# Expert weights in rows of 8192 bytes, a ring of 12 places, and the next gather ahead of the down projection

## Chip, cores and metric

The kernel runs on one core of one Trainium2 chip. The metric is the device time of one execution in microseconds (us).

## The reference

One decoder layer on 256 tokens of 2048 features, all in float32. The part that the change touches is the channel half, a mixture of 32 experts in 4 groups: each token takes its best group and the two best experts in it.

```python
def hier_moe(h, w_grp, w_exp, w1, w3, w2):
    ht = h.reshape(-1, D)                                   # 256 x 2048
    pg = softmax(ht @ w_grp); g_sel = argmax(pg); p_g = max(pg)
    el_sel = logits (ht @ w_exp) of the 8 experts of g_sel
    top_p, top_i = lax.top_k(softmax(el_sel), 2)
    top_w = top_p / sum(top_p) * p_g                        # combine: 256 x 32, two entries a row
    for e in range(32):
        a = jax.nn.silu(ht @ w1[e]) * (ht @ w3[e])          # w1, w3: 2048 x 512
        y = y + combine[:, e:e + 1] * (a @ w2[e])           # w2: 512 x 2048
```

Ahead of it stand adaLN conditioning (`c` times a 2048 x 12288 matrix), an input projection, sparse attention beside a pooling branch, and an output projection. The three expert arrays are 384 MiB of the 554 MB that the core reads.

## The kernel before

Everything up to the router runs in stages: adaLN sums on VectorE, projections on TensorE, attention, pooling, the output projection with the router's logits built block by block (`route_block`, L530 to L566). Then L574 to L649 select experts and give each token a slot (at most 32 tokens, `CAP`, per expert) with each of its experts.

The experts run four at a time (`quad`, L663, eight calls at L801). One quad has these steps. **Gather**: VectorE builds a 0/1 matrix `gq` (L666 to L669); TensorE multiplies the tokens `x1c` with it (L676) into PSUM tiles of two banks (`banks`, tag `b2`, two of them); VectorE scales them into `xg` (L680). **Hidden**: for each block `kb` of 256 features and for `w1` and `w3`, two loads of 1 MiB bring 256 rows of two experts each (L694), and 8 float32 matmuls follow, four experts side by side in column groups of 32 (L699; the trace has two records for each matmul); the two results stand in the two one-bank PSUM tiles `mm`. **Turn**: SiLU, product, four transposes (L706 to L712). **Down** (`cols`): for 1024 output columns, over four blocks `f` of 128 hidden features, two loads of 1 MiB (two experts, 1024 columns each, L721) and 16 matmuls (L726). **Combine**: times the gate (L732), back to the tokens through `gwT` (L735, into `b2` tiles), added onto the residual `xs` (L737). The last quad takes its columns as 1024, 512, 256, 256 and stores each piece.

A load of weights needs a free place. `moe_w` (L655) hands places out: 13 of `FIRST_SLOTS` for the first 13 loads, then a ring of the 8 `MOE_SLOTS`. A place comes free when the last matmul that reads it is done. SyncE (SP) issues all weight loads in one fixed order and stands still at one whose place isn't free. The order on each engine is set when the kernel is built, by a list scheduler that may take a ready instruction ahead of one that waits; a tile's release follows all its readers.

In HBM an expert's `w1` row (512 floats) is 2048 bytes, and a partition takes two neighbouring rows (`r=2`), so a DMA row is 4096 bytes; of `w2` it is 1024 columns, also 4096 bytes. The order of features within `xg`, `x1c`, `wr`, `sc2T` and `sh2T` follows this `r`.

```python
    MOE_SLOTS = [(t, one) for t in ("Pq", "Pp", "H1")] + [("w", wp)] * 4 + [("H0", one)]
    FIRST_SLOTS = MOE_SLOTS + [("B8", one), ("acc", rot)] + [("f", fp)] * 3
```

Of the kernel before, what the change touches and what calls it, by code (L numbers as in the profile page):

```python
# [9 lines left out]
F32 = mybir.dt.float32  # L10
# [6 lines left out]
P = 128  # L17
# [17 lines left out]
CAP = 32  # L35
QE = 4
# [41 lines left out]
def layer_kernel(ctx: ExitStack, tc: tile.TileContext, x, c, w_ada, b_ada, norm1_g, w_in, q_norm_g,  # L78
# [20 lines left out]
    MOE_SLOTS = [(t, one) for t in ("Pq", "Pp", "H1")] + [("w", wp)] * 4 + [("H0", one)]  # L99
    FIRST_SLOTS = MOE_SLOTS + [("B8", one), ("acc", rot)] + [("f", fp)] * 3  # L100
# [97 lines left out]
    vb2 = one.tile([24, 256], F32, name="vb2")  # L198
    nc.sync.dma_start(vb2[0:8], norm2_g[0].rearrange("(k n) -> k n", n=256))
    nc.sync.dma_start(vb2[8:24], b_ada[3 * D:5 * D].rearrange("(k n) -> k n", n=256))  # L200
    pt = bank([P, 2, 24], "sm")
    for r in range(2):
        nc.tensor.transpose(pt[:, r], vb2.rearrange("k (q r) -> k r q", r=2)[:, r], ident[0:24, 0:24])
    v2T = one.tile([P, 24, 2], F32, name="v2T")
# [32 lines left out]
    def vec_end(acc, bias, gain, name):  # L237
        av = acc.rearrange("p (k q r) -> p k r q", q=P, r=2)
        pt = bank([P, KC], "fl")
        for k in range(KC):  # L240
            nc.tensor.matmul(pt[:, k:k + 1], lhsT=av[:, k // 2, k % 2], rhs=ones[:, 0:1], start=True, stop=True)  # L241
# [10 lines left out]
    def fill_steps():  # L252
        v2 = lambda j: v2T[:, 8 * j:8 * j + 8].rearrange("p k r -> p (k r)")
# [259 lines left out]
    wr = one.tile([P, 8, 2, 36], F32, name="wr")  # L513
    for r in range(2):
        nc.sync.dma_start(wr[:, :, r, 0:NE], w_exp.rearrange("(k p r) e -> p k r e", p=P, r=2)[:, :, r])
        nc.sync.dma_start(wr[:, :, r, NE:36], w_grp.rearrange("(k p r) e -> p k r e", p=P, r=2)[:, :, r])
# [11 lines left out]
    x1c = one.tile([P, NT, 8, 2, P], F32, tag="N", name="x1c")  # L528

    def route_block(n):  # L530
        if n == 3:
            while "sh2T" not in results:
                fill(1)
            sh2T = results["sh2T"]
            pb = bank([P, 36], "sm")
            for k in range(KC):
                nc.tensor.matmul(pb, lhsT=sh2T[:, k:k + 1].to_broadcast([P, P]), rhs=wr[:, k // 2, k % 2],
                                 start=(k == 0), stop=(k == KC - 1))
            nc.vector.tensor_copy(brt, pb)
        for i in range(NT):  # L540
            t = t2()
            nc.scalar.activation(t, xs[:, i, n * 512:(n + 1) * 512], AF.Square, accum_out=ss2[:, i, n:n + 1])
        xv = xs[:, :, n * 512:(n + 1) * 512].rearrange("p i (k q r) -> p i k r q", q=P, r=2)
        for i in range(NT):
            nc.scalar.copy(x1c[:, i, 2 * n:2 * n + 2], xv[:, i])
        pt = banks([P, 4, S])
        for u in range(4):
            for i in range(NT):
                nc.tensor.transpose(pt[:, u, i * P:(i + 1) * P], xv[:, i, u // 2, u % 2], ident)
        h = r4([P, 4, S])  # L550
        for u in range(4):
            k = n * 4 + u
            if u % 2:
                nc.vector.tensor_scalar(h[:, u], pt[:, u], sc2T[:, k:k + 1], None, op0=ALU.mult)
            else:
                nc.scalar.activation(h[:, u], pt[:, u], AF.Copy, scale=sc2T[:, k:k + 1])
        pl = bank([P, NT, 36], "sm")
        for i in range(NT):
            for u in range(4):
                k = n * 4 + u  # L560
                nc.tensor.matmul(pl[:, i], lhsT=h[:, u, i * P:(i + 1) * P], rhs=wr[:, k // 2, k % 2],  # L561
                                 start=(u == 0), stop=(u == 3))
# [100 lines left out]
    def quad(e0, last):  # L663
# [7 lines left out]
        for kq in range(2):  # L671
            px = banks([P, 8, QS])
            for u in range(8):
                k = kq * 8 + u
                for i in range(NT):
                    nc.tensor.matmul(px[:, u], lhsT=x1c[:, i, k // 2, k % 2],  # L676
                                     rhs=gq[:, i].rearrange("p e s -> p (e s)"), start=(i == 0), stop=(i == NT - 1))
# [8 lines left out]
        if e0 == 0:  # L686
            fill(100)
        hs = [bank([P, DE], "mm") for _ in range(2)]
        for kb in range(KC // 2):
            for wx, h in ((w1, hs[0]), (w3, hs[1])):  # L690
                ws = []
                for e in range(0, QE, 2):
                    w = moe_w([P, 2, 2, DE])
                    nc.sync.dma_start(w, wx[e0 + e:e0 + e + 2, kb * 256:(kb + 1) * 256, :].rearrange("e (p r) n -> p e r n", r=2))  # L694
                    ws += [w[:, 0], w[:, 1]]
                for r in range(2):
                    k = kb * 2 + r
# [14 lines left out]
        nc.vector.tensor_copy(aT, pa)  # L712

        def cols(c0, width):
# [14 lines left out]
            for n in range(0, width, 512):  # L729
                m = min(512, width)  # L730
                y = t2()
                nc.vector.tensor_mul(y[:, 0:m], py[:, n:n + m], gt2[:, c0 + n:c0 + n + m])  # L732
                pz = banks([P, NT, 512])
                for i in range(NT):
                    nc.tensor.matmul(pz[:, i, 0:m], lhsT=gwT[:, i], rhs=y[:, 0:m], start=True, stop=True)  # L735
                xv = xs[:, :, c0 + n:c0 + n + m]
                nc.vector.tensor_add(xv, xv, pz[:, :, 0:m])  # L737
                if last:
                    nc.scalar.dma_start(out[:, c0 + n:c0 + n + m].rearrange("(i p) n -> p i n", p=P), xv)

        cols(0, 1024)
        if last:
            cols(1024, 512)
            cols(1536, 256)
            cols(1792, 256)
        else:
            cols(1024, 1024)

# [1 line left out]
    def overflow():  # L750
        gt2 = results["gt2"]
        h2 = []
        for hf in range(2):
            h2T = slot([P, 8, S], FILL_SLOTS)
            x1n = wtile([P, NT, 8, P])
            for i in range(NT):
                nc.vector.tensor_scalar(x1n[:, i], x1c[:, i, hf * 4:hf * 4 + 4].rearrange("p k r q -> p (k r) q"), rs2[:, i:i + 1], None, op0=ALU.mult)
# [9 lines left out]
        with tc.For_i(0, NE, 1) as ev:  # L767
# [69 lines left out]
```

## Time and profile before

| | us |
|---|---|
| median of 3 runs | 1453.95 |
| lowest, highest | 1449.43, 1456.39 |
| span of the profiled execution | 1453.5 |
| TensorE busy in it | 1097.4 |
| VectorE busy in it | 476.8 |
| mean DMA rate over it | 383 GB/s |

The profile cuts the span into 40 slices of 36 us. Up to slice 12 TensorE and VectorE are busy; from slice 14 (about 500 us) on the experts run, and the DMA rate stands near 405 GB/s up to the last slices. The chain of work that ended last is for 57% of the span a load of expert weights.

### The profile page before, as it was taken

Reading aid. Unit: us, or ns where it says so; the run is one execution under the profiler, and the core shown is the slowest. Engines: PE = TensorE matmul, PEld = TensorE weight load, DVE = VectorE, ACT = ScalarE, POOL = GpSimd, SP = SyncE. Lnnn points to the kernel's source line nnn. Section 1 sums busy time; section 2 is a strip of 40 time slices with the busy share of each in tenths; the row PEclk is TensorE's granted clock in tenths of the full one; section 3 lists DMA queues with packets and bytes.
Section 4 is the critical chain, followed back from the end, with each engine's and each line's share of the span. In section 5 each row is a group of like instructions: output and inputs, shape, how many; then the busy total and the mean of one; then the engine's idle time right before and its main releaser. Section 6 shows DMA issues by size and latency. Waiting matters only on the chain.

```text
span 1453.5 us, 12826 instructions
## 1 busy us (share of the span) xinstructions
PE 1097.4 (75%) x5165; PEld 418.2 (29%) x5165; DVE 476.8 (33%) x815; ACT 99.7 (7%) x230; POOL 0.2 (0%) x4
## 2 busy tenths in 40 slices
PE   2999999999995867656867755675685677668655
PEld 1444444655564113111311311131131131113111
DVE  5876678996767003001201200210120021012002
ACT  3200002441220000000000000000000000000000
POOL 0000000000000000000000000000000000000000
PEclk9999999999976889999989999999999998899897
DMA  9999999999987999999999999999999999999997
GB/s 305 372 386 358 369 347 351 373 355 376 406 334 270 374 404 401 409 407 404 404 409 404 405 409 409 405 400 409 408 406 409 407 404 389 408 399 384 410 398 258
DMA packets 171968, 557.29 MB, mean 383 GB/s; under 512 B 15129, under 2 KB 29433, under 8 KB 163457
## 3 DMA queue, kind: packets, MB, share of 16 engines
q1 hardware_dynamic: 170544, 554.32, 98.5%
q10 hardware_dynamic: 1360, 2.10, 0.4%
q8 instruction: 43, 0.70, 0.2%
q14 instruction: 21, 0.16, 0.0%
HBM read 554.29 MB, written 2.10 MB: 383 GB/s over the span
## 4 chain that ended last, share of the span: by engine, by line
DMA 60%; PE 35%; DVE 4%; ACT 1%; issue 1%; SPq 0%; DVEq 0%
DMA w<-in_w_dram 57%; PE mm L395 11%; PE mm L503 8%; PE mm L699 6%; PE b L726 3%; DVE bacc L160 2%; DMA w<-in_w_ada_dram 1%; PE b L676 1%; DVE acc L160 1%; PE fl L233 1%; PE fl L232 1%; DMA w<-in_w_in_dram 1%; PE b L735 1%; PE fl L241 1%; PE sm L561 1%
## 5 line engine op out<-in xcount | busy, mean ns | idle before, releaser
L699 PE MATMUL mm<-w,xg 128*32 128x512 f32 x2048 | 364.2, 653 | 181.9 <-DMA w<-in_w_dram 181.9
L726 PE MATMUL b<-w,t 128*32 128x512 f32 (+1 forms) x1056 | 188.8, 642 | 98.6 <-DMA w<-in_w_dram 92.3
L395 PE MATMUL mm<-w,hT 128*128 128x512 f32 (+1 forms) x512 | 208.3, 563 | 3.2 <-ACT hT L386 1.7
L699 PEld LDWEIGHTS mm<-w,xg 128*32 128x32 f32 x2048 | 72.6, 113 | 467.1 <-DMA w<-in_w_dram 287.8
L707 DVE TENSOR_TENSOR t<-t,mm 128x512 f32<-128x512 f32 x8 | 5.5, 688 | 534.6 <-PE mm L699 470.1
L160 DVE SCALAR_TENSOR_TENSOR acc<-w,sT,acc 128x2048 f32<-128x2048 f32 x60 | 140.7, 2345 | 1.1 <-DMA w<-in_w_ada_dram 1.0
L395 PEld LDWEIGHTS mm<-w,hT 128*128 128x128 f32 x512 | 92.3, 193 | 106.4 <-issue 98.8
L732 DVE TENSOR_TENSOR t<-b,gt 128x512 f32<-128x512 f32 (+1 forms) x33 | 20.9, 671 | 269.7 <-PE b L726 269.7
L726 PEld LDWEIGHTS b<-w,t 128*32 128x32 f32 x1056 | 35.7, 113 | 242.4 <-DMA w<-in_w_dram 182.0
L160 DVE SCALAR_TENSOR_TENSOR bacc<-w,sT,bacc 128x512 f32<-128x512 f32 (+1 forms) x150 | 94.3, 643 | 10.8 <-DMA w<-in_w_ada_dram 8.0
L735 PE MATMUL b<-t,gwT 128*128 128x512 f32 (+1 forms) x132 | 62.5, 616 | 13.8 <-DVE t L732 13.8
L706 ACT ACTIVATE t<-mm 128x512 f32<-128x512 f32 x8 | 4.8, 597 | 865.5 <-PE mm L699 865.5
L676 PE MATMUL b<-gq,x1c 128*128 128x128 f32 x512 | 60.9, 282 | 1.7 <-DVE gq L669 1.7
L676 PEld LDWEIGHTS b<-gq,x1c 128*128 128x128 f32 x512 | 60.1, 198 | 2.1 <-DVE gq L669 2.1
L503 PE MATMUL mm<-w,mixA 128*128 128x512 f32 x128 | 59.3, 617 | 0.0
L503 PE MATMUL mm<-w,mixP 128*128 128x512 f32 x128 | 56.2, 592 | 0.0
L680 DVE TENSOR_SCALAR xg<-b,sc2T,sh2T 128x128 f32<-128x128 f32 x128 | 42.3, 404 | 24.2 <-PE b L676 24.2
L737 DVE TENSOR_TENSOR xs<-xs,b 128x1024 f32<-128x1024 f32 (+1 forms) x33 | 39.2, 1188 | 30.9 <-PE b L735 30.9
L735 PEld LDWEIGHTS b<-t,gwT 128*128 128x128 f32 x132 | 24.6, 197 | 55.7 <-DVE t L732 32.9
L503 PEld LDWEIGHTS mm<-w,mixA 128*128 128x128 f32 x128 | 24.6, 198 | 28.0 <-issue 28.0
L503 PEld LDWEIGHTS mm<-w,mixP 128*128 128x128 f32 x128 | 24.0, 190 | 27.4 <-issue 27.0
L401 DVE TENSOR_TENSOR pqkv<-pqkv,mm 128x512 f32<-128x512 f32 x24 | 16.5, 686 | 18.0 <-PE mm L395 17.9
(208 smaller groups left out, 459.1 us busy)
## 6 DMA issues: line engine op xcount, KB each, us to landing
w<-in_w_dram SPq DMA_DIRECT2D x380, 1024.0 KB, 16.7
w<-in_w_ada_dram SPq DMA_DIRECT2D x96, 1024.0 KB, 8.3
w<-in_w_in_dram SPq DMA_DIRECT2D x21, 1024.0 KB, 7.2
w<-in_w_out_dram SPq DMA_DIRECT2D x16, 1024.0 KB, 8.3
w<-in_w_in_dram SPq DMA_DIRECT2D x14, 512.0 KB, 8.7
w<-in_w_dram SPq DMA_DIRECT2D x8, 512.0 KB
xs<-in_x_dram SPq DMA_DIRECT2D x2, 1024.0 KB, 7.9
out_dram<-xs ACTq DMA_DIRECT2D x3, 512.0 KB, 8.4
```

The costliest lines, as they stand in the source:

```text
L160: nc.vector.scalar_tensor_tensor(acc, w[:, kk], sT[:, k:k + 1], acc, op0=ALU.mult, op1=ALU.add)
L232: nc.tensor.matmul(pt, lhsT=ones, rhs=acc[:, n * 512:(n + 1) * 512], start=True, stop=False)
L395: nc.tensor.matmul(po[:, :width], lhsT=hTs[k // 8][:, k % 8, i * P:(i + 1) * P], rhs=w[:, j], start=(j == 0), stop=(j == nk - 1))
L401: nc.vector.tensor_add(d, d, po[:, :width])
L503: nc.tensor.matmul(po, lhsT=mix[:, k, i * P:(i + 1) * P], rhs=ws[k // 4][:, k % 4], start=(k == 0), stop=(k == 7))
L676: nc.tensor.matmul(px[:, u], lhsT=x1c[:, i, k // 2, k % 2], rhs=gq[:, i].rearrange("p e s -> p (e s)"), start=(i == 0), stop=(i == NT - 1))
L680: nc.vector.tensor_scalar(xg[:, k], px[:, u], sc2T[:, k:k + 1], sh2T[:, k:k + 1], op0=ALU.mult, op1=ALU.add)
L699: nc.tensor.matmul(h[e * CAP:(e + 1) * CAP, :], lhsT=xg[:, k, e * CAP:(e + 1) * CAP], rhs=ws[e][:, r], start=(k == 0), stop=(k == KC - 1), ...
L726: nc.tensor.matmul(py[e * CAP:(e + 1) * CAP, nw], lhsT=aT[:, f, e * CAP:(e + 1) * CAP], rhs=ws[e][:, nw], start=(f == 0), stop=(f == 3), s ...
L732: nc.vector.tensor_mul(y[:, 0:m], py[:, n:n + m], gt2[:, c0 + n:c0 + n + m])
L735: nc.tensor.matmul(pz[:, i, 0:m], lhsT=gwT[:, i], rhs=y[:, 0:m], start=True, stop=True)
L737: nc.vector.tensor_add(xv, xv, pz[:, :, 0:m])
```

## The change

- `RB = 4`: a partition takes four neighbouring rows of `w1` and `w3`, so one load of 1 MiB is 512 rows of one expert, in DMA rows of 8192 bytes; a step of `hidden` is four loads and 16 matmuls, for twice as many features. All tensors in the order of features follow (`x1c`, `wr`, `v2T`, `vec_end`, `route_block`); the router's weights come in eight loads, not four.
- `down` loads whole rows of `w2` (2048 columns, 8192 bytes) of one expert, four loads a step, and keeps both `b2` tiles for the sums of all 2048 columns; `combine` then uses the `mm` banks for its products. The last quad (`down_last`) keeps its column pieces and their loads.
- The ring has 12 places: the 8, three places `f` and one `acc`.
- `gather` of the next quad stands between `hidden` and `down` of this one.

```diff
+RB = 4
-    MOE_SLOTS = [(t, one) for t in ("Pq", "Pp", "H1")] + [("w", wp)] * 4 + [("H0", one)]
-    FIRST_SLOTS = MOE_SLOTS + [("B8", one), ("acc", rot)] + [("f", fp)] * 3
+    MOE_SLOTS = [(t, one) for t in ("Pq", "Pp", "H1")] + [("w", wp)] * 4 + [("H0", one)] + [("f", fp)] * 3 + [("acc", rot)]
+    FIRST_SLOTS = MOE_SLOTS[:8] + [("B8", one), ("acc", rot)] + [("f", fp)] * 3
...
-        xv = xs[:, :, n * 512:(n + 1) * 512].rearrange("p i (k q r) -> p i k r q", q=P, r=2)
-        for i in range(NT):
-            nc.scalar.copy(x1c[:, i, 2 * n:2 * n + 2], xv[:, i])
+        xv = xs[:, :, n * 512:(n + 1) * 512].rearrange("p i (q r) -> p i r q", q=P, r=RB)
+        for i in range(NT):
+            nc.scalar.copy(x1c[:, i, n], xv[:, i])
...
-        for kb in range(KC // 2):
+    def hidden(e0, xg):
         hs = [bank([P, DE], "mm") for _ in range(2)]
+        for kb in range(KC // RB):
             for wx, h in ((w1, hs[0]), (w3, hs[1])):
                 ws = []
-                for e in range(0, QE, 2):
-                    w = moe_w([P, 2, 2, DE])
-                    nc.sync.dma_start(w, wx[e0 + e:e0 + e + 2, kb * 256:(kb + 1) * 256, :].rearrange("e (p r) n -> p e r n", r=2))
-                    ws += [w[:, 0], w[:, 1]]
-                for r in range(2):
-                    k = kb * 2 + r
+                for e in range(QE):
+                    w = moe_w([P, RB, DE])
+                    nc.sync.dma_start(w, wx[e0 + e, kb * RB * P:(kb + 1) * RB * P, :].rearrange("(p r) n -> p r n", r=RB))
+                    ws.append(w)
+                for r in range(RB):
+                    k = kb * RB + r
...
+    def combine(py, c0, m, gwT, store):
+        gt2 = results["gt2"]
+        y = t2()
+        nc.vector.tensor_mul(y[:, 0:m], py, gt2[:, c0:c0 + m])
+        for i in range(NT):
+            pz = bank([P, 512], "mm")
+            nc.tensor.matmul(pz[:, 0:m], lhsT=gwT[:, i], rhs=y[:, 0:m], start=True, stop=True)
+            xv = xs[:, i, c0:c0 + m]
+            nc.vector.tensor_add(xv, xv, pz[:, 0:m])
...
+    def down(e0, aT, gwT):
+        py = [banks([P, 1024]) for _ in range(2)]
+        for f in range(4):
+            ws = []
+            for e in range(QE):
+                w = moe_w([P, D])
+                nc.sync.dma_start(w, w2[e0 + e, f * P:(f + 1) * P, :])
+                ws.append(w)
+            for n in range(4):
+                for e in range(QE):
+                    nc.tensor.matmul(py[n // 2][e * CAP:(e + 1) * CAP, (n % 2) * 512:(n % 2 + 1) * 512],
...
+        for n in range(4):
+            combine(py[n // 2][:, (n % 2) * 512:(n % 2 + 1) * 512], n * 512, 512, gwT, False)
...
+    xg, gwT = gather(0)
+    fill(100)
     for q in range(NQ):
-        quad(q * QE, q == NQ - 1)
+        a = hidden(q * QE, xg)
+        if q == 0:
+            gate_end(5, results["gt2 sums"], "gt2")
+        held = gwT
+        if q + 1 < NQ:
+            xg, gwT = gather((q + 1) * QE)
+            down(q * QE, turned(a), held)
+        else:
+            down_last(q * QE, turned(a), held)
```

## Rows read from the trace of the kernel before

**Rows 1.** The page: busy time; granted clock, DMA share, DMA rate over 40 slices.

```profile
PE 1097.4 (75%) x5165; PEld 418.2 (29%) x5165; DVE 476.8 (33%) x815; ACT 99.7 (7%) x230; POOL 0.2 (0%) x4
...
PEclk9999999999976889999989999999999998899897
DMA  9999999999987999999999999999999999999997
GB/s 305 372 386 358 369 347 351 373 355 376 406 334 270 374 404 401 409 407 404 404 409 404 405 409 409 405 400 409 408 406 409 407 404 389 408 399 384 410 398 258
```

**Rows 2.** The chain that ended last: start us, us, what.

```profile
606.03 1.94 PE mm L699 x12
...
626.51 1.94 PE mm L699 x12
...
689.06 1.94 PE b L726 x12
...
1312.19 3.60 PE b L726 x12
```

**Rows 3.** The page: DMA issues of expert weights, count, KB each, us to landing.

```profile
w<-in_w_dram SPq DMA_DIRECT2D x380, 1024.0 KB, 16.7
...
w<-in_w_dram SPq DMA_DIRECT2D x8, 512.0 KB
```

**Rows 4.** DMA packets of three stretches: 84 to 96, 720 to 780, 410 to 418 us.

```profile
DMA packets 2624, 4.62 MB, mean 385 GB/s; under 512 B 475, under 2 KB 475, under 8 KB 2609
...
DMA packets 6356, 24.54 MB, mean 409 GB/s; under 512 B 371, under 2 KB 371, under 8 KB 6354
...
DMA packets 503, 3.40 MB, mean 425 GB/s; under 512 B 52, under 2 KB 52, under 8 KB 123
```

**Rows 5.** Busy time by stretch: PE, PEld, DVE, ACT, POOL, PEclk, DMA share, GB/s.

```profile
468.00:488.00 20.00, 18.65 (x88) 4.91 (x86) 0.00 (x0) 2.34 (x4) 0.00 (x0) 0.87 1.01 401
488.00:493.00 5.00, 5.00 (x44) 1.34 (x40) 0.00 (x0) 0.00 (x0) 0.00 (x0) 0.85 0.53 137
...
702.00:709.00 7.00, 6.96 (x60) 2.33 (x58) 2.98 (x9) 0.00 (x0) 0.00 (x0) 1.00 0.98 382
...
949.00:960.00 11.00, 10.58 (x87) 4.43 (x86) 4.63 (x15) 0.00 (x0) 0.00 (x0) 1.00 0.97 374
1076.00:1081.00 5.00, 4.73 (x43) 1.14 (x32) 1.62 (x6) 0.00 (x0) 0.00 (x0) 1.00 1.01 380
1199.00:1208.00 9.00, 8.56 (x75) 3.76 (x78) 3.86 (x12) 0.00 (x0) 0.00 (x0) 1.00 0.87 323
1325.00:1334.00 9.00, 9.00 (x84) 4.50 (x86) 4.37 (x14) 0.00 (x0) 0.00 (x0) 1.00 0.83 301
```

**Rows 6.** TensorE in order of time: start us, us, line, count, idle before.

```profile
463.59 6.20 PE L699 MATMUL mm<-w,xg 128*32 128x512 f32 x52
...
691.76 3.70 PE L735 MATMUL b<-t,gwT 128*128 128x512 f32 x8 [0.79 <-DVE t L732]
...
702.76 6.20 PE L699 MATMUL mm<-w,xg 128*32 128x512 f32 x52
```

**Rows 7.** Groups by line: count, busy us, mean ns, idle before.

```profile
L676 PE MATMUL b<-gq,x1c 128*128 128x128 f32 x512 | 60.9, 282 | 1.7 <-DVE gq L669 1.7
...
L680 DVE TENSOR_SCALAR xg<-b,sc2T,sh2T 128x128 f32<-128x128 f32 x128 | 42.3, 404 | 24.2 <-PE b L676 24.2
...
L732 DVE TENSOR_TENSOR t<-b,gt 128x512 f32<-128x512 f32 x31 | 20.0, 686 | 263.0 <-PE b L726 263.0
...
L549 PE MATMUL b<-kc,xs 128*128 128x128 f32 x32 | 5.9, 314 | 0.0
...
L545 ACT COPY x1c<-xs 128x512 f32<-128x512 f32 x8 | 5.3, 660 | 32.5 <-DVE xs L508 32.5
```

**Rows 8.** Two stretches of one ring round; columns as in Rows 5.

```profile
714.00:719.00 5.00, 4.09 (x16) 0.72 (x16) 0.00 (x0) 0.00 (x0) 0.00 (x0) 0.66 1.03 410
719.00:722.00 3.00, 1.91 (x12) 0.39 (x12) 0.00 (x0) 0.00 (x0) 0.00 (x0) 1.00 1.02 408
```

More of the change, by code (lines that the diff above doesn't have):

```diff
@@ L237, in vec_end @@
     def vec_end(acc, bias, gain, name):
-        av = acc.rearrange("p (k q r) -> p k r q", q=P, r=2)
+        av = acc.rearrange("p (k q r) -> p k r q", q=P, r=RB)
         pt = bank([P, KC], "fl")
         for k in range(KC):
-            nc.tensor.matmul(pt[:, k:k + 1], lhsT=av[:, k // 2, k % 2], rhs=ones[:, 0:1], start=True, stop=True)
+            nc.tensor.matmul(pt[:, k:k + 1], lhsT=av[:, k // RB, k % RB], rhs=ones[:, 0:1], start=True, stop=True)
         v = one.tile([P, KC], F32, name=name)
@@ L511, in out_proj @@
             fill(3)
[L513 to L516, printed above, removed]
+    wr = one.tile([P, KC // RB, RB, 36], F32, name="wr")
+    for k in range(KC // RB):
+        nc.sync.dma_start(wr[:, k, :, 0:NE], w_exp.rearrange("(k p r) e -> k p r e", p=P, r=RB)[k])
+        nc.sync.dma_start(wr[:, k, :, NE:36], w_grp.rearrange("(k p r) e -> k p r e", p=P, r=RB)[k])
     out_proj(mixP, 8, "wo_pool")
@@ L527, in layer_kernel @@
     brt = one.tile([P, 36], F32, name="brt")
-    x1c = one.tile([P, NT, 8, 2, P], F32, tag="N", name="x1c")
+    x1c = one.tile([P, NT, KC // RB, RB, P], F32, tag="N", name="x1c")
     def route_block(n):
@@ L536, in route_block @@
             for k in range(KC):
-                nc.tensor.matmul(pb, lhsT=sh2T[:, k:k + 1].to_broadcast([P, P]), rhs=wr[:, k // 2, k % 2],
+                nc.tensor.matmul(pb, lhsT=sh2T[:, k:k + 1].to_broadcast([P, P]), rhs=wr[:, k // RB, k % RB],
                                  start=(k == 0), stop=(k == KC - 1))
@@ L560, in route_block @@
                 k = n * 4 + u
-                nc.tensor.matmul(pl[:, i], lhsT=h[:, u, i * P:(i + 1) * P], rhs=wr[:, k // 2, k % 2],
+                nc.tensor.matmul(pl[:, i], lhsT=h[:, u, i * P:(i + 1) * P], rhs=wr[:, k // RB, k % RB],
                                  start=(u == 0), stop=(u == 3))
@@ L661, in layer_kernel, with gather @@
     QS = QE * CAP
-    def quad(e0, last):
+    def gather(e0):
         gq = rot.tile([P, NT, QE, CAP], F32, tag="gq", name="gq")
@@ L675, in quad @@
                 for i in range(NT):
-                    nc.tensor.matmul(px[:, u], lhsT=x1c[:, i, k // 2, k % 2],
+                    nc.tensor.matmul(px[:, u], lhsT=x1c[:, i, k // RB, k % RB],
                                      rhs=gq[:, i].rearrange("p e s -> p (e s)"), start=(i == 0), stop=(i == NT - 1))
@@ L712, in quad, with down_last @@
         nc.vector.tensor_copy(aT, pa)
-        def cols(c0, width):
+        return aT
+    def combine(py, c0, m, gwT, store):
[7 more added lines that the diff above has]
+            nc.vector.tensor_add(xv, xv, pz[:, 0:m])
+        if store:
+            nc.scalar.dma_start(out[:, c0:c0 + m].rearrange("(i p) n -> p i n", p=P), xs[:, :, c0:c0 + m])
+    def down(e0, aT, gwT):
[9 more added lines that the diff above has]
+                    nc.tensor.matmul(py[n // 2][e * CAP:(e + 1) * CAP, (n % 2) * 512:(n % 2 + 1) * 512],
+                                     lhsT=aT[:, f, e * CAP:(e + 1) * CAP], rhs=ws[e][:, n * 512:(n + 1) * 512],
+                                     start=(f == 0), stop=(f == 3), skip_group_check=True,
+                                     tile_position=(0, e * CAP))
+        for n in range(4):
+            combine(py[n // 2][:, (n % 2) * 512:(n % 2 + 1) * 512], n * 512, 512, gwT, False)
+    def down_last(e0, aT, gwT):
+        for c0, width in ((0, 1024), (1024, 512), (1536, 256), (1792, 256)):
             py = banks([P, width])
@@ L730, in cols @@
                 m = min(512, width)
-                y = t2()
-                nc.vector.tensor_mul(y[:, 0:m], py[:, n:n + m], gt2[:, c0 + n:c0 + n + m])
-                pz = banks([P, NT, 512])
-                for i in range(NT):
[L735 to L747, printed above, removed]
+                combine(py[:, n:n + m], c0 + n, m, gwT, True)
     def overflow():
```

34 lines of the change are left out of this document (16 added, 18 removed).

## The prediction

> **What bounds the kernel now.** I read the page's slices first [rows 1]: from slice 14 on the DMA digit is 9 and the rate stays near 405 GB/s, while TensorE and VectorE have gaps. The chain of waits [rows 2] shows the pace: the same step recurs after 626.51 - 606.03 = 20.48 us, of which TensorE's step takes 1.94 and the wait for loads the rest. That is one round of the ring, eight loads of 1 MiB: 2.56 us a load, and 8 x 1,048,576 bytes in 20.48 us is 409.6 GB/s, the rate that the packets of an undisturbed stretch show [rows 4] in their middle line. The expert stage is bound by the DMA engines themselves, in rows of 4096 bytes. From 689.06 to 1312.19 the end of the down projection recurs five times, 124.6 us a quad, where 48 loads at 2.56 us are 122.9; so five quads lose 8.7 us somewhere. The stretches around the quads' ends [rows 5] say where: four have a DMA share below the usual 1.02 (0.98, 0.97, 0.87, 0.83), the queue ran dry; another (1076 to 1081) has share 1.01 at 380 GB/s, busy but slow.
>
> **Longer rows.** What does one row cost an engine? In a stretch of nearly pure 2048-byte rows the rate is 385 GB/s [rows 4]: 16 x 2048 / 385 = 85.1 ns a row. At 4096 bytes: 16 x 4096 / 409 = 160.2 ns. The second 2048 bytes cost 75.1 ns, so about 10.0 ns of each row don't depend on its length, and a row of 8192 bytes should take 10 + 4 x 75.1 = 310 ns, 422 GB/s. The trace has such rows, of the adaLN weights: in 410 to 418 us, 380 of 503 packets, 3.11 of 3.40 MB, are 8192 bytes long, and the rate is 425 GB/s [rows 4], which is about 308 ns, a saving of 12 for each pair of 4096-byte rows. But the stretch is 8 us long, and no long one of these rows alone exists. I take 10 ns, bounds 0 (no row shows it over a long stream) and 12. A load of 1 MiB is 128 such rows, 8 on each engine: 80 ns saved, 2.56 to 2.48 us. There are 380 + 8 issues [rows 3]: 256 loads of w1 and w3 and 112 of w2 get long rows; the last quad's 16 MiB of w2 keep theirs. Of the 368, the first 13 go to the starting places while other work sets the pace, and save nothing: 355 x 0.08 = **28.4 us** (0 to 34.1).
>
> [...]
>
> **Twelve places, at the start.** TensorE begins the experts at 463.59 and has a backlog; between 488 and 493 the DMA share is 0.53 at 137 GB/s [rows 5], because the 8 ring loads issued before had landed and nothing was free. That is 5 x (1 - 137/409) = 3.3 us. Four more places are 4 x 2.48 = 9.9 us of further loads, which covers it: **-3.3** (0 to 3.3). They need no other wait: the `f` and `acc` places were used by the first 13 loads and come free in turn. Against it: a step now reads four loads, so the first place comes free after 32 matmul records, not 16; at 6.20 us for 52 [rows 6] that is 16 x 0.119 = **+1.9** (0 to 1.9; the queue is dry then, and SP, which issues everything in order, stands in front of it).
>
> **The moved gather.** It issues no DMA and is moved past none on SP; on TensorE its 64 records (60.9 / 8 = 7.6 us) and on VectorE its 16 scalings (42.3 / 8 = 5.3 us) [rows 7] go ahead of the down projection's work. Before, TensorE takes no weights from 691.0 (689.06 + 1.94) to 702.76 [rows 2, 6], 11.8 us: combine, then gather, which needs the same `b2` banks. After, gather can run in TensorE's gaps of `hidden`, since both `b2` tiles are then free; what remains at the end is combine. It now uses the `mm` banks, so the next `hidden`, queued behind it on TensorE, waits for the last addition: 4 products of 0.686 us and 8 additions of the same shape, taken at the same time, are 8.2 us of VectorE [rows 7], the first of them under the last matmuls. Does the queue run dry meanwhile? When the last group of four lands, eight places are in flight, 19.8 us, and the four just landed come free within some 4 us and add 9.9. TensorE is back after 4 + 8.2 us and needs 4 us for the next group: about 16 of 29.7. If the scheduler leaves gather where the code has it, its 7.6 us stand ahead of the down projection and meet the same slack. So the dry time goes: (1.02 - share) / 1.02 over the four stretches is 0.27 + 0.54 + 1.32 + 1.68 = **3.8 us** (0, to 8.7 if the busy but slow stretches go as well, for which I see no reason).
>
> **TensorE and the router.** A step is 32 records in 9.9 us of loading. [...] The router now reads `xs` with a step of four floats, not two, in 8 copies of 660 ns on ScalarE and 32 transposes of 314 ns [rows 7]; no row shows the new step's price. Between nothing and double for the last block alone, which is on the path (2 copies, 8 transposes, 3.8 us), I take **+1.0**, as its neighbours at the old step are near other copies' times. The four extra small router loads and the reordered vectors lie early under other work: nothing, and some tenths if that cover is gone. In the last quad only the additions are split in two; nothing.
>
> Sum: -28.4 - 3.3 + 1.9 - 3.8 + 1.0 = -32.6. Against the profiled span, 1453.5 - 32.6 = 1420.9; the median of the runs is 0.45 above that span, so 1421.
>
> **The rivals.**
> [...]
> 2. *The start goes wrong.* The ring's `acc` place shares its two buffers with the last adaLN sums, and the scheduler fixes SP's order: a load that waits for that place holds all behind it. The sums' reader, `gate_end`, stands behind the first `hidden` in the code; half a ring round dry, 10 us, once: 1431. 0.08.
> 3. *Slower: long rows collide in HBM.* All rows of a load now lie in one contiguous MiB, read by 16 engines at once. If that makes long stretches like 1076 to 1081 (380 GB/s with the engines busy) the rule, a load takes 2.76 us: 355 x 0.2 = +71, and with the other terms 1521. The other terms give 4.2 us, so it is slower than before once a load costs 12 ns more than 2.56, below 407.7 GB/s, and by over 0.5% below some 405. Against it: w2 is read at the same distance of rows now, and the round's 20.48 us holds for the stage. 0.04.
> [...]
> 5. *It doesn't do what it says*: rows stay 4096 bytes; only the ring and gather act: 1449. 0.02.
> 6. *More*: everything at its upper bound, and below 1406: 0.03.
>
> **How the numbers follow.** The forecast's case has 0.68 (1406 to 1431). The range must reach the first rival: 1406 to 1440. At the low end stand 34.1 + 3.3 + 8.7 = 46.1, 1408; at the high end the first rival. About 0.5%, 7 us, is what a measurement of this kernel can tell from no change. Faster than that (under 1446.7): 0.68 + 0.12 + 0.08 + 0.03 = 0.91; slower: 0.05 of rivals 3 and 4; same: 0.04.
>
> **What would show it.** Loads recur at 2.48 us in the chain, 422 GB/s by stretches; a quad lasts 119 to 120 us; no stretch around a quad's end has a DMA share below 1.0; the stretch at 488 to 493 is full; L676 runs between L699's matmuls. Wrong if the rate stays at 409, if SP stands still around 470 to 490, or if the granted clock is low through the stage.

## The result and the profile after

| | before | after |
|---|---|---|
| median, us | 1453.64 | 1437.28 |
| lowest, highest, us | 1449.43, 1456.39 | 1435.75, 1438.30 |
| profiled span, us | 1453.5 | 1434.8 |
| first `hidden` matmul on TensorE, us | 463.59 [rows 6] | 473.09 |
| from there to the end, us | 989.9 | 961.7 |

The changed kernel takes 0.9882 of the time before (95% interval 0.9858 to 0.9906): faster, inside the range, and 16 us above the forecast of 1421. The last two lines of the table are the key to the rest: the experts start 9.5 us later (both times from one profiled execution each), and what follows is 28.2 us shorter.

The page of the changed kernel answers to [rows 1, 3]: busy time, granted clock and DMA rate over 40 slices, and the loads of expert weights.

```profile
PE 1170.3 (82%) x5167; PEld 457.1 (32%) x5167; DVE 481.7 (34%) x848; ACT 103.5 (7%) x230; POOL 0.2 (0%) x4
...
PEclk9999999999986887989988999999998899899888
...
GB/s 298 372 386 382 362 343 356 369 366 377 328 301 309 340 421 279 422 421 421 421 421 421 421 421 422 421 421 421 421 421 421 421 421 421 421 421 421 421 407 277
...
w<-in_w_dram SPq DMA_DIRECT2D x380, 1024.0 KB, 19.1
```

From slice 15 on the rate is 421 or 422 in every slice but one, up to the last two; before, the slices went up and down between 384 and 410. One slice, the sixteenth (538 to 574 us), has 279. And slices 11 to 14 (359 to 502 us) sum to less than before (328 + 301 + 309 + 340 against 406 + 334 + 270 + 374): that is the late start.

The chain that ended last (start us, us, what), in answer to [rows 2]:

```profile
692.63 19.82 DMA w<-in_w_dram
...
712.52 19.83 DMA w<-in_w_dram
```

The DMA packets of 720 to 780 us, in answer to [rows 4]:

```profile
DMA packets 3477, 25.31 MB, mean 422 GB/s; under 512 B 390, under 2 KB 390, under 8 KB 390
```

Eight loads take 712.52 - 692.63 = 19.89 us, 2.49 a load (2.48 was forecast), and the rate is the 422 that the line through the shorter rows gave.

Windows of the changed kernel, columns as in Rows 5: the quads' stage, the end of the first long quad in it, and the stretches where time was lost.

```profile
600.00:1350.00 750.00, 587.44 (x2917) 174.41 (x2918) 95.83 (x205) 3.58 (x6) 0.00 (x0) 0.93 1.01 421
...
706.00:718.00 12.00, 11.94 (x53) 3.84 (x52) 7.50 (x13) 0.00 (x0) 0.00 (x0) 1.00 1.02 421
...
556.00:572.00 16.00, 14.15 (x112) 8.12 (x115) 6.21 (x18) 0.59 (x1) 0.00 (x0) 0.96 0.31 98
472.00:480.00 8.00, 8.00 (x63) 2.98 (x65) 3.46 (x11) 0.00 (x0) 0.00 (x0) 1.00 0.27 80
350.00:360.00 10.00, 10.00 (x29) 6.94 (x30) 3.84 (x5) 0.59 (x1) 0.00 (x0) 0.63 1.03 424
360.00:370.00 10.00, 10.00 (x22) 4.34 (x21) 2.96 (x3) 0.00 (x0) 0.00 (x0) 0.86 0.48 191
```

The first line is the gain: 421 GB/s over 750 us with the DMA share at 1.01; in the kernel before it is 404 over the same window. The second is a quad's end, where four of [rows 5] ran dry: share 1.02. The third is a hole in the weight stream that the kernel before doesn't have, 16 x (1 - 98/422) = 12.3 us at full rate. Of the last three, the stretch at 472 to 480 has its like in the kernel before, at 464 to 468 us (19 GB/s); the other two belong to the late start.

### The hole at 556 to 572

TensorE in order of time around it (start us, us, line, tiles, count, idle before and its releaser):

```profile
528.48 3.62 PE L701 MATMUL mm<-w,xg 128*32 128x512 f32 x26 [1.43 <-DMA w<-in_w_dram]
539.61 2.07 PE L234 MATMUL fl<-t,ones 1*128 1x512 f32 x2 [7.51 <-DMA t<-in_b_ada_dram]
542.36 2.08 PE L233 MATMUL fl<-acc,ones 128*128 128x512 f32 x2 [0.68 <-ACT gt L235]
...
551.28 5.06 PE L677 MATMUL b<-gq,x1c 128*128 128x128 f32 x22
556.13 1.61 PE L233 MATMUL fl<-acc,ones 128*128 128x512 f32 x2
557.57 4.85 PE L677 MATMUL b<-gq,x1c 128*128 128x128 f32 x42
...
565.76 14.12 PE L739 MATMUL b<-w,t 128*32 128x512 f32 x104 [1.84 <-DVE t L714]
```

What SP issued there:

```profile
523.52 5.15 SPq L231 DMA_DIRECT2D t<-in_b_ada_dram  x3
530.99 11.22 SPq L735 DMA_DIRECT2D w<-in_w_dram  x7
542.30 0.25 SPq L231 DMA_DIRECT2D t<-in_b_ada_dram  x1
557.77 0.33 SPq L696 DMA_DIRECT2D w<-in_w_dram  x1
569.41 1.89 SPq L735 DMA_DIRECT2D w<-in_w_dram  x4
```

Two of SP's waits of 380 to 600 us (waited for: us in total, times, longest):

```profile
SPq L696 <- PE fl L233: 14.4, 1, 14.4
SPq L735 <- PE b L739: 11.4, 1, 11.4
```

Read together: the first `hidden` ends at 528.48 + 3.62 = 532.1, and the first matmul of the down projection is at 565.76. For 33.7 us TensorE uses no weights, so no place comes free, and SP, after the seven loads up to 542.2, issues one in 27 us. The time goes to `gate_end` and to the second gather. `gate_end` needs four bias rows of 2 KB; three of them are issued at 523.52, behind the weight loads in flight, and TensorE waits for them until 539.61; the fourth is issued at 542.30, behind seven more loads. Before, SP issued these rows at 448 to 452, ahead of the queue. And one of the ring's places is `acc`, which the last gate matmul (556.13 + 1.61 = 557.74) sets free: SP stands for it for 14.4 us and issues at 557.77.

### The late start

TensorE's matmuls of `vec_end`, which turns a row of adaLN sums into the order of features, by group (count, busy us, mean ns); before, L241:

```profile
L241 PEld LDWEIGHTS fl<-ones,acc 128*128 128x128 f32 x64 | 9.0, 214 | 1.4 <-issue 1.4
L241 PE MATMUL fl<-ones,acc 128*128 128x1 f32 x64 | 8.5, 261 | 0.0
```

and after, L242, with the router's copies and transposes that answer to [rows 7]:

```profile
L242 PEld LDWEIGHTS fl<-ones,acc 128*128 128x128 f32 x64 | 15.7, 329 | 1.7 <-issue 1.5
L242 PE MATMUL fl<-ones,acc 128*128 128x1 f32 x64 | 14.8, 359 | 0.0
...
L546 ACT COPY x1c<-xs 128x512 f32<-128x512 f32 x8 | 9.0, 1125 | 36.7 <-DVE xs L509 36.7
...
L550 PE MATMUL b<-kc,xs 128*128 128x128 f32 x32 | 6.2, 329 | 0.0
```

The operand `av[:, k // RB, k % RB]` is read with a step of four floats, two before. A weight load takes 329 ns instead of 214, and the one-column matmul behind it doesn't hide it: 14.8 us instead of 8.5, +6.3. Then the clock: in the same stretch the kernel before has

```profile
350.00:360.00 10.00, 10.00 (x38) 5.72 (x39) 4.90 (x5) 0.59 (x1) 0.00 (x0) 1.00 1.00 386
360.00:370.00 10.00, 10.00 (x25) 4.48 (x24) 8.85 (x7) 1.30 (x3) 0.00 (x0) 1.00 1.01 405
```

while the changed one was granted 0.63 and 0.86 (above), with 0.50 over 354 to 362 us. The fall begins while 32 records of these slow matmuls run (347.5 to 357.2). The 44 projection records of the attention half that follow take 21.93 us instead of 19.13, +2.8. TensorE is busy all through these stretches (20.00 of 20 us over 350 to 370), so both sums land on the start of the experts: 6.3 + 2.8 = 9.1, most of the 9.5 us.

ScalarE's copies of the router, with the step of four floats too, take 1125 ns instead of 660 [rows 7]; the transposes there take 329 instead of 314. So the weight loads and the copies take longer with the wider step and the transposes hardly; why, no run shows.

### The profile page after: what moved, and what is told of

Read it like the earlier page. It is cut to its first block, busy times and chain, and to the rows that moved or that the text cites. A ratio compares the mean times of both kernels' runs of the same rounds, so it can differ in the third digit from the quotient of the medians.

```text
span 1434.8 us, 12818 instructions
## 1 busy us (share of the span) xinstructions
PE 1170.3 (82%) x5167; PEld 457.1 (32%) x5167; DVE 481.7 (34%) x848; ACT 103.5 (7%) x230; POOL 0.2 (0%) x4
## 4 chain that ended last, share of the span: by engine, by line
DMA 53%; PE 6%; DVE 0%; issue 0%; SPq 0%; DVEq 0%
DMA w<-in_w_dram 53%; PE mm L701 3%; PE b L677 2%; PE b L739 1%; PE b L759 0%; PE mm L723 0%; DVE t L706 0%; DVE xg L681 0%; SPq L696 0%; PE sm L684 0%; PE sm L712 0%; SPq L735 0%; DVE t L720 0%; DVE xs L725 0%; DVE t L714 0%
## 5 line engine op out<-in xcount | busy, mean ns | idle before, releaser
L701 PE MATMUL mm<-w,xg 128*32 128x512 f32 x2048 | 398.6, 710 | 151.7 <-DMA w<-in_w_dram 151.6
L701 PEld LDWEIGHTS mm<-w,xg 128*32 128x32 f32 x2048 | 87.3, 125 | 448.3 <-DMA w<-in_w_dram 273.8
L739 PE MATMUL b<-w,t 128*32 128x512 f32 x896 | 187.4, 598 | 35.5 <-DMA w<-in_w_dram 28.9
L686 DVE COPY gwT<-sm 128x256 f32<-128x256 f32 x8 | 3.4, 424 | 377.7 <-PE sm L684 377.7
L739 PEld LDWEIGHTS b<-w,t 128*32 128x32 f32 x896 | 46.2, 109 | 172.6 <-issue 84.1
L677 PE MATMUL b<-gq,x1c 128*128 128x128 f32 x512 | 66.4, 291 | 1.7 <-DVE gq L670 1.7
L677 PEld LDWEIGHTS b<-gq,x1c 128*128 128x128 f32 x512 | 63.6, 205 | 12.8 <-issue 10.7
L723 PE MATMUL mm<-t,gwT 128*128 128x512 f32 (+1 forms) x132 | 63.9, 614 | 1.6 <-DVE t L720 1.1
L725 DVE TENSOR_TENSOR xs<-xs,mm 128x512 f32<-128x512 f32 (+1 forms) x66 | 44.2, 670 | 21.9 <-PE mm L723 21.7
L723 PEld LDWEIGHTS mm<-t,gwT 128*128 128x128 f32 x132 | 21.6, 192 | 44.1 <-DVE xs L725 28.4
L504 PEld LDWEIGHTS mm<-w,mixA 128*128 128x128 f32 x128 | 25.8, 208 | 29.9 <-issue 29.9
L504 PEld LDWEIGHTS mm<-w,mixP 128*128 128x128 f32 x128 | 24.0, 190 | 27.4 <-issue 27.0
## 6 DMA issues: line engine op xcount, KB each, us to landing
w<-in_w_dram SPq DMA_DIRECT2D x380, 1024.0 KB, 19.1
```

What stands on the lines that cost most here:

```text
L504: nc.tensor.matmul(po, lhsT=mix[:, k, i * P:(i + 1) * P], rhs=ws[k // 4][:, k % 4], start=(k == 0), stop=(k == 7))
L677: nc.tensor.matmul(px[:, u], lhsT=x1c[:, i, k // RB, k % RB], rhs=gq[:, i].rearrange("p e s -> p (e s)"), start=(i == 0), stop=(i == NT - 1))
L701: nc.tensor.matmul(h[e * CAP:(e + 1) * CAP, :], lhsT=xg[:, k, e * CAP:(e + 1) * CAP], rhs=ws[e][:, r], start=(k == 0), stop=(k == KC - 1), ...
L723: nc.tensor.matmul(pz[:, 0:m], lhsT=gwT[:, i], rhs=y[:, 0:m], start=True, stop=True)
L725: nc.vector.tensor_add(xv, xv, pz[:, 0:m])
L739: nc.tensor.matmul(py[n // 2][e * CAP:(e + 1) * CAP, (n % 2) * 512:(n % 2 + 1) * 512], lhsT=aT[:, f, e * CAP:(e + 1) * CAP], rhs=ws[e][:, ...
```

## The experiments

Medians of four to ten runs each; the ratio is to the kernel before on the same chip (1454.27, 1454.45 and 1454.84 us).

| run | built on | edit | median, us | ratio (95%) | span |
|---|---|---|---|---|---|
| e1_gate_first | after | `gate_end` ahead of the first `hidden` | 1427.82 | 0.9816 (0.9791 to 0.9841) | 1426.5 |
| e2_no_acc | after | ring of 11, no `acc` | 1440.71 | 0.9902 (0.9878 to 0.9925) | 1439.9 |
| e3_vec_copy | after | `vec_end` reads contiguous copies | 1434.16 | 0.9871 (0.9840 to 0.9901) | 1432.8 |
| e5_both | after | e1 and e3 | 1422.55 | 0.9790 (0.9760 to 0.9819) | 1419.5 |
| e10_gate_after_gather | e5 | gate's matmuls queued behind the first gather | 1423.57 | 0.9769 (0.9740 to 0.9799) | 1423.5 |
| e6_ring8 | e5 | ring of 8 | 1431.97 | 0.9844 (0.9815 to 0.9873) | 1427.8 |
| e7_gather_back | e5 | next gather behind `down` | 1423.33 | 0.9772 (0.9743 to 0.9801) | 1423.2 |
| e8_ring8_gather_back | e5 | both | 1461.87 | 1.0046 (1.0028 to 1.0064) | 1460.9 |
| e11_rows_4k | e5 | rows of 4096 bytes | 1451.73 | 0.9981 (0.9964 to 0.9997) | 1445.3 |
| e9_before_ring12 | before | ring of 12 alone | 1443.98 | 0.9938 (0.9917 to 0.9959) | 1439.4 |

### What makes the hole: e1 and e2

```diff
     fill(100)
+    gate_end(5, results["gt2 sums"], "gt2")
     for q in range(NQ):
         a = hidden(q * QE, xg)
-        if q == 0:
-            gate_end(5, results["gt2 sums"], "gt2")
```

> The changed kernel, with gate_end(5) called ahead of the first hidden. Theory: the 12 us without DMA at 556 to 572 us come from TensorE standing at the gate's matmuls from 532 to 566 us, because their bias rows were issued on SP behind the weight loads; then the stretch is full and the time is 1437 - 12 = 1425. Rival: the ring's place acc, which waits for the sums, is the cause; moved forward, the gate frees it as well, so this run alone gives 1425 under both, and the next one tells them apart. Third: the stall only moves to the start of the stage, where TensorE then pays the 10 us of gate work: 1435 to 1437.

```diff
-    MOE_SLOTS = [...] + [("f", fp)] * 3 + [("acc", rot)]
+    MOE_SLOTS = [...] + [("f", fp)] * 3
```

> The changed kernel with 11 places, without acc; gate_end where it was. If the wait for acc holds up SP, the hole at 556 to 572 us goes: 1425. If TensorE's absence does, the hole stays and begins one load (2.5 us) sooner: 1437 to 1440.

Measured: with the gate first, 9.5 us faster than the changed kernel; without the `acc` place, 3.4 us slower. Of the 12.3 us of the hole, 8.3 show in the span (1434.8 to 1426.5): the gate's first matmuls now stand ahead of the experts, which start at 475.26 and not at 473.09. The window of the hole with the gate first:

```profile
556.00:572.00 16.00, 13.11 (x46) 2.85 (x42) 0.00 (x0) 0.00 (x0) 0.00 (x0) 1.00 1.01 420
```

its window without the `acc` place:

```profile
553.00:571.00 18.00, 16.15 (x117) 8.67 (x119) 6.21 (x18) 0.59 (x1) 0.00 (x0) 0.89 0.15 45
```

and the wait of SP that fills it there:

```profile
SPq L735 <- PE b L739: 28.9, 2, 27.4
```

So the hole goes when the gate's rows are issued early (457.8 to 462.1 us in e1) and TensorE is back at the weights 4.5 us after the last `hidden` matmul (540.87 to 545.40), not 33.7. How much of it the rows alone would mend is not shown: no run issues them early and leaves the gate's matmuls where they were. Taking the `acc` place away only changes for whom SP waits: 27.4 us in one wait for the first matmuls of the down projection. The wait for `acc` that the trace of after shows is real and last in its place, but not the cause.

### What makes the start late: e3, e10

```diff
-        for k in range(KC):
-            nc.tensor.matmul(pt[:, k:k + 1], lhsT=av[:, k // RB, k % RB], ...)
+        for kb in range(KC // RB):
+            t = t2([P, RB, P])
+            nc.scalar.copy(t, av[:, kb])
+            for r in range(RB):
+                k = kb * RB + r
+                nc.tensor.matmul(pt[:, k:k + 1], lhsT=t[:, r], ...)
```

> The changed kernel, with the two column sums of vec_end read from contiguous copies, made by ScalarE in 512 columns at a time. Theory: TensorE's weight loads with a step of four floats (64 records, 14.8 us against 8.5 before) and the slower clock behind them put the stage's start from 463.6 to 473.1 us; then it is back at 464 and the time is 1437 - 9 = 1428. Rival: the later start comes from the router's copies and transposes, which are unchanged here: 1435 to 1437.

Measured: 3.1 us faster by the medians, 1.6 by the ratios, whose intervals overlap, so by itself this is hardly told from no change; it is not the whole of the loss. Between e1 and e5, on one chip, the same edit is worth 5.3 us by the medians and 3.8 by the ratios. The groups of this kernel:

```profile
L243 ACT COPY t<-acc 128x512 f32<-128x512 f32 x8 | 8.6, 1137 | 0.7 <-DVE xs L513 0.7
L246 PEld LDWEIGHTS fl<-ones,t 128*128 128x128 f32 x64 | 8.1, 204 | 0.5 <-issue 0.5
L246 PE MATMUL fl<-ones,t 128*128 128x1 f32 x64 | 8.1, 256 | 0.0
```

and TensorE's wait ahead of the router's counts, with its first `hidden` matmul:

```profile
456.67 2.08 PE L233 MATMUL fl<-acc,ones 128*128 128x512 f32 x2 [13.89 <-DVE acc L161]
...
472.41 7.93 PE L705 MATMUL mm<-w,xg 128*32 128x512 f32 x72
```

The price of the step is confirmed by its absence: 204 ns a load, 8.1 us in all. But the lower clock stayed (below, at e5), and the planner now puts the first gate matmul ahead of the router's work on TensorE, where it stands 13.89 us for the last adaLN sums of VectorE, and the experts start at 472.41 all the same. Is that wait the new bound, or is VectorE? The next kernel has both repairs (e5, below), with the gate's matmuls queued behind the first gather (`last_gather` holds the last matmul of a gather):

```diff
-    gate_end(5, results["gt2 sums"], "gt2")
+    with tc.issue_after(last_gather[0].ins):
+        gate_end(5, results["gt2 sums"], "gt2")
```

> As e5_both, with the gate's matmuls queued on TensorE behind the first gather. Theory: in e3_vec_copy and e5_both TensorE stood 13.9 us at the first of them, for the last adaLN sums, ahead of the router's counts; without that the experts start at 464 us, as in the kernel before, and not at 469: 1422.5 - 5 = 1417. Rival: the last sums on VectorE hold up the router as well: 1421 to 1423.

Its order on TensorE, at the last `vec_end` matmuls and at the start:

```profile
357.69 4.27 PE L246 MATMUL fl<-ones,t 128*128 128x1 f32 x32
361.82 9.83 PE L508 MATMUL mm<-w,mixA 128*128 128x512 f32 x16
...
458.08 0.61 PE L628 MATMUL sm<-mem,kc 128*128 128x32 f32 x2 [16.05 <-DVE c L645]
...
473.49 3.64 PE L707 MATMUL mm<-w,xg 128*32 128x512 f32 x32
```

The long wait is still there, 16.05 us, now in front of the router's counts and for VectorE's result there. The median is 1.0 us from e5's, and the intervals of the ratios overlap. So TensorE's queue order is not what is left of the late start; the sums and the router share VectorE, and what VectorE does in those 16 us is shown below, at e5.

### Both repairs: e5

> The changed kernel with gate_end(5) first and vec_end from contiguous copies. If both losses are what the theory says and add up: 1437 - 12 - 9 = 1416, which would be the forecast without its two errors (1421 less 5 us of stretches that were busy but slow). If they overlap: 1422 to 1428.

Edits of e1 and e3 together: 1422.55 us, 14.7 below the changed kernel and the fastest of all kernels here. TensorE at the same places as in e10:

```profile
356.15 3.63 PE L246 MATMUL fl<-ones,t 128*128 128x1 f32 x32
359.64 7.11 PE L508 MATMUL mm<-w,mixA 128*128 128x512 f32 x16
...
451.91 2.08 PE L233 MATMUL fl<-acc,ones 128*128 128x512 f32 x2 [13.89 <-DVE acc L161]
...
469.38 3.64 PE L705 MATMUL mm<-w,xg 128*32 128x512 f32 x32
```

and the window of the quads' stage:

```profile
600.00:1350.00 750.00, 586.21 (x2917) 173.41 (x2916) 95.88 (x205) 3.58 (x6) 0.00 (x0) 0.94 1.01 421
```

The experts start at 469.38, 5.8 us later than before and 3.7 earlier than after. From 456 to 473 us the weight stream stands (3 GB/s over that window), the starting places being full, so a later start is time lost. VectorE in order of time, the first and the last of four adaLN sums, and the router's matmuls with the shift vector on TensorE:

```profile
441.14 2.34 DVE L161 SCALAR_TENSOR_TENSOR acc<-w,sT,acc 128x2048 f32<-128x2048 f32 x1
...
449.50 2.35 DVE L161 SCALAR_TENSOR_TENSOR acc<-w,sT,acc 128x2048 f32<-128x2048 f32 x1
...
423.03 6.88 PE L542 MATMUL sm<-wr,sh2T 128*128 128x36 f32 x32
```

Four of the last sums (441.14, 443.99, 446.74, 449.50) stand among the router's steps on VectorE, between the last logits and the counts; in the kernel before it is one (436.02), and the others come later. So TensorE has 16.04 us from its last logits matmul (438.02) to the counts (454.06), where before it had 9.87 (435.39 to 445.26): +6.2. From the counts to the first `hidden` matmul it is then 15.32 instead of 18.33: -3.0. The other +2.6 lie ahead of the last logits matmul. In e10 four sums stand at the same place (445.17 to 453.52). The trace shows this order; no run changes it alone.

Some of the start is chance. The same 16 records after the same 32 one-column records take 7.11 us here, at a granted clock of 1.00, and 9.83 in e10, at 0.66 (360 to 370 us). Of the seven kernels with contiguous copies, e5 and e11 kept the full clock in their profiled execution, e3, e6, e7 and e10 took 9.5 to 10.1 us for these records, and e8 8.81. So this fall of the clock is not tied to the slow reads alone: at the first run of one-column matmuls it is there in some kernels' profiled executions and not in others, and is worth up to 3 us. It was there in after, e1 and e2 (0.61 to 0.63 over 350 to 360 us), and in neither before nor the ring of 12 on it (e9), whose 32 records stand in two runs of 2.17 and 1.70 us with other work between (in after too there is other work between, but the two runs take 4.13 and 3.23). Behind the second 32 records of this kind e5 and e11 lost time as well. The clock was 0.50 over 406 to 409 us in before and over 415 to 420 in after; over 410 to 420 it was 0.54 in e1, 0.51 in e2 and 0.81 in e5; in e9 the page has the digit 8 for the slice of 396 to 432 us, after three of 9. The 32 records of L542, which stand behind that run in e5 (423.03), take 6.88 us there and 6.9 in the other six kernels with contiguous copies, where before and after have 3.66.

### Ring and gather: e6, e7, e8, e9

e6 takes the last four places from the ring (`[("f", fp)] * 3 + [("acc", rot)]`) and e8 does so too; e7 and e8 swap two lines:

```diff
-            xg, gwT = gather((q + 1) * QE)
             down(q * QE, turned(a), held)
+            xg, gwT = gather((q + 1) * QE)
```

> As e5_both, with the ring of 8 places; rows of 8192 bytes and the early gather stay. When the last group of a quad lands, 4 loads are in flight (9.9 us) and 4 places come free about 4 us later: 19.8 us of cover against TensorE's absence of about 16 us. If the early gather is enough by itself: 1422 to 1426. If 8 places are too few for steps of four loads: a hole at each of 7 ends of a quad, 5 us or more each, 1457 and up.

> As e5_both, with the gather of the next quad behind the down projection, as in the kernel before; 12 places and rows of 8192 bytes stay. TensorE then takes no weights for about 22 us at the end of a quad, against 29.7 us of cover: if 12 places are enough by themselves, 1422 to 1425. If the move is what filled the dry stretches: at least the 4 us that they were, 1427 and up.

> As e5_both, with both the ring of 8 places and the gather behind the down projection: rows of 8192 bytes alone. 19.8 us of cover against 26 us until the next group of places is free: a hole of about 6 us at each of 7 ends, 1422.5 + 43 = 1465, slower than the kernel before. If the cover is better than that: 1425 to 1435, rows alone would do.

| median, us | gather ahead of `down` | gather behind it |
|---|---|---|
| ring of 12 | 1422.55 | 1423.33 |
| ring of 8 | 1431.97 | 1461.87 |

With 12 places the moved gather is worth nothing that can be measured; with 8 it is worth 29.9. Four more places are worth 9.4 (7.9 by the ratios) with the early gather and 38.5 with the late one. With neither, the long rows make the kernel slower than before. e6 met neither of its two cases: its experts start 1.9 us later than e5's (471.29), and its quads' stage runs at 418 GB/s and not 421, some 5 us over 750, so eight places with the early gather lose a little at each quad's end and not 5 us. Where e8 loses, its page shows (rate over 40 slices):

```profile
GB/s 298 375 386 354 376 346 352 373 351 386 395 368 174 391 421 420 360 421 421 356 422 421 364 412 422 421 355 421 422 355 423 421 421 355 422 421 356 421 395 286
```

and its window of one quad's end:

```profile
706.00:718.00 12.00, 11.36 (x98) 5.67 (x96) 6.21 (x18) 0.00 (x0) 0.00 (x0) 1.00 0.56 216
```

Mostly 420 to 423 between the dips, and seven dips, one for each of the first seven quads' ends: in the one shown, 12 x (1 - 216/422) = 5.9 us at full rate. A step now takes four places at once, so eight places are two steps, and combine and gather together outlast them.

The ring alone, on the kernel before with its rows of 4096 bytes:

```diff
-    MOE_SLOTS = [...] + [("H0", one)]
+    MOE_SLOTS = [...] + [("H0", one)] + [("f", fp)] * 3 + [("acc", rot)]
```

> The kernel before, with the ring of 12 places alone (the three places f and acc added): rows of 4096 bytes, gather behind the down projection. If the ring is worth what its dry stretches were, 3.3 us at 488 to 493 and 3.8 us at the ends of quads: 1454 - 7 = 1447. If the busy but slow stretches go too: 1442. If acc's wait for the last adaLN sums holds up SP at the start: 1450 to 1460.

Its rate over 40 slices:

```profile
GB/s 309 372 386 367 380 345 351 374 353 386 400 348 270 411 396 408 409 405 404 410 409 409 409 409 409 410 409 409 409 409 409 409 408 409 410 407 409 409 397 246
```

10.9 us faster than before (by the ratio 0.0062 x 1454.84 = 9.0), and the slices of the second half lie flat at 409: the dry stretches and the busy but slow one of [rows 5] went together, by places alone. (The profiled execution is 14.1 us shorter: 10.2 of them lie between the first `hidden` matmul and the end, 989.9 to 979.7, and 3.9 are an earlier start.)

### Rows: e11

```diff
-                    nc.sync.dma_start(w, wx[...].rearrange("(p r) n -> p r n", r=RB))
+                    src = wx[...].rearrange("(p r) n -> p r n", r=RB)
+                    for hv in range(2):
+                        nc.sync.dma_start(w[:, 2 * hv:2 * hv + 2], src[:, 2 * hv:2 * hv + 2])
```

(and `w2` in two halves of 1024 columns the same way)

> As e5_both, but each load of 1 MiB is issued as two of 512 KB, the halves of its rows: DMA rows of 4096 bytes into the same places, in the same order for TensorE. Only the row length (and the count of issues) is undone. If a pair of rows costs 10 ns more than one long row: 355 loads x 0.08 us = +28, 1451, at 409 GB/s through the stage. [...]

The window of the quads' stage, and the DMA packets of 720 to 780 us:

```profile
600.00:1350.00 750.00, 595.14 (x2858) 167.76 (x2854) 95.83 (x205) 3.58 (x6) 0.00 (x0) 0.95 1.03 409
```

```profile
DMA packets 6740, 24.57 MB, mean 409 GB/s; under 512 B 749, under 2 KB 749, under 8 KB 6738
```

Same places, same order, same matmuls, only the row is halved: 29.2 us slower than e5 by the medians, 0.0191 x 1454 = 27.8 by the ratios (the two intervals together leave some 5 us either way) and 26.1 from the first `hidden` matmul to the end in the two profiled executions (976.2 against 950.1), at 409 GB/s instead of 421. It also doubles the number of issues, which could be part of it; that the packets of 720 to 780 give the same 409 as those of before, where issues were single, speaks against.

## Why the prediction was right, and where it was not

**What bounds the kernel, and longer rows: right.** 28.4 was forecast, 26 to 29 measured by e11, with the rate of a long stream at 422 GB/s as the straight line through two row lengths gave it. The 425 of the 8 us stretch was a little high. The term of the first rival, a smaller saving, to which 0.12 and the high end of the range go, is shown by no run: the runs show 26 to 29 us in its place. The third, collisions in HBM, falls at 421 GB/s over 750 us.

**Dry stretches at quads' ends: right, and too small.** 3.8 was taken, with 8.7 if the busy but slow stretches went as well, "for which I see no reason". They went, in after and in e9. What ended them was the places; why 1076 to 1081 was slow with its engines busy (380 GB/s at a share of 1.01 [rows 5]) stays open.

**The moved gather.** L677 does run between the matmuls of `hidden`, and five quads take 119.9 us each (706.11 to 1305.59 between the same matmuls of combine), inside the forecast's 119 to 120. The reckoning that with 12 places the slack covers gather wherever it stands was right too (e7). One sentence of it was wrong: the count of places in flight. A load lands 19.1 us after its issue at 2.49 us a load, so some 8 are in flight, not 12; the other places hold landed weights. They still bridge the end of a quad.

**Twelve places at the start.** -3.3: the stretch of [rows 5] at 488 to 493 is full after the change (424 GB/s over 480 to 493). The dry one at 472 to 480 is not new: before, it lay at 464 to 468 (19 GB/s), right after TensorE's first `hidden` matmul as here. +1.9 for the first step of four is there in part: SP issues again 2.8 us after that matmul before (466.40), 4.5 after it in the changed kernel (477.60) and 3.7 in e5 (473.03), so 0.8 to 1.7.

**The router: two terms changed places.** +1.0 was taken for the block on the path; from the end of the last `vec_end` matmuls on (406.26 before, 415.49 after) the way to the first `hidden` matmul is 57.33 and 57.60 us, so +0.3. The step that failed is the next sentence: "the reordered vectors lie early under other work: nothing, and some tenths if that cover is gone". They lie early, but on TensorE, which has no slack there: +6.3, and up to +2.8 by the clock that falls behind them. The price of the strided read was looked for in the router's copies and transposes alone; the same step stood in `vec_end`, in front of one-column matmuls that did not hide it (14.8 us for 64 records instead of 8.5).

**The second rival had the place, not the mechanism.** "The start goes wrong", 10 us dry, once, with 0.08: the hole is 12.3 us, once. Its mechanism was the `acc` place, and SP does stand 14.4 us for it; but without that place the hole stays (e2). The cause is `gate_end`'s four bias rows behind megabytes of weights, and TensorE away from the weights for gate and gather in a row (e1, which mends both at once). The forecast's check of the moved gather, "it issues no DMA and is moved past none on SP", looked at gather and not at its neighbour, whose DMAs the new order let slip from 448 to 523 us. One of the forecast's own signs failed there: "no stretch around a quad's end has a DMA share below 1.0", and at the first quad's end it is 0.31.

**The sum.** -32.6 was forecast. That 1437 lies within 1406 to 1440 is luck: the forecast's own case ended at 1431, and the part above that was added to reach the first rival, long rows that save less, whose term no run shows. What filled it are two losses that the sum put at +1.0 or at nothing. With the hole and the slow reads repaired, the span is 34.0 shorter (e5), and the median 1422.55 against 1421. That agreement has two errors in it that cancel: the start is 5.8 later where 1.0 was allowed (in an execution that kept its clock at the first `vec_end`), and from the start to the end e5 takes 1419.5 - 469.4 = 950.1, which is 39.8 less than before, where 33.6 was forecast. Of the 39.8, the rows are 26.1 (e11) and the places 10.2 (e9), by the same measure. In the changed kernel itself it is 9.5 for the start, 12.3 for the hole and, as what is left of the span's difference, 40.5 saved: -18.7.

**The granted clock** was not low through the stage: its mean over 600 to 1350 us is 0.93, and TensorE is busy for 587.44 of the 750 us, so its steps stay under their loads. With that **the fourth rival**, counted with the slower cases, falls. **The fifth** too: 8192-byte rows are there (of 3477 packets of 720 to 780 us, 390 are shorter).

**What stays open.** Whether the 5.8 us later start of e5 can be had back. e10 shows that TensorE's order does not mend it, and the traces show four sums instead of one among the router's steps on VectorE; the planner moves sums, router and gate against each other at every edit, and no run held the sums back.

## What to carry to other kernels

Price a changed access pattern at every instruction that reads through it, and ask of each whether its engine has slack there, above all of weight loads ahead of short matmuls: here 329 ns a load instead of 214, and +6.3 us. When an order is changed, list the small DMAs of the neighbours as well: the three rows of 2 KB that went out behind weight loads of 1 MiB held their reader some 16 us (523.52 to 539.61 in after), and the hole that they are part of cost the weight stream 12.3. Larger groups needed more places here: with groups of four loads, 8 places instead of 12 cost 9.4 us (e6) and, with the late gather, 38.5 (e8). Count them in groups, not in loads.

## What the runs showed of the hardware

- The cost of a DMA row is a straight line in its length here: about 10 ns and 75 ns for each 2048 bytes, an estimate from 385 and 409 GB/s at 2048 and 4096 bytes [rows 4], which the 422 GB/s of 720 to 780 us in after (8192 bytes) met.
- A weight load of 128 x 128 in `vec_end` took 329 ns with a step of four floats (after, e1, e2), 214 and 198 with a step of two (before, e9), 193 to 212 from contiguous copies (e3 204); the router's 128-column transposes hardly show the step (a matmul 329 ns against 314 [rows 7], its weight load 220 in after against 213 in before).
- TensorE's granted clock fell at a run of 32 records of one-column matmuls although the engine's busy time has no gap there: to 0.63 and 0.86 over two stretches of 10 us in after, to 0.66 over one in e10, not at all in e5 and e11, whose order on TensorE is the same at that place. Around the second such run of 32 it fell as well: to 0.50 over 406 to 409 us in before and over 415 to 420 in after, to 0.81 over 410 to 420 in e5. There is one profile of each kernel, and no run separates what decides it.
- SP waited for the landing of an earlier load at 206 of the issues at L696 in after (402.0 us in all): with 12 places, some 8 loads were in flight (19.1/2.49 = 7.7; before, 16.7 [rows 3] over 2.56 = 6.5 with 8 places). In e11, with loads half as large, it is 10.2 us to landing at 1.28 us a load (512 KB at 409 GB/s): again 8 loads, and half the bytes. Whether the chip or the program sets that count, no run shows.
